# Modulation columns summed on VectorE instead of TensorE, past the first four chunks of layer 0

## The chip, the cores and the metric

One core of a Trainium2 chip runs the whole program. The metric is device time in microseconds (us) of one execution; lower is better. The profile is of one execution on the same kind of chip, with its own time beside it. TensorE does the matrix products (PE in the profile, and PEld for its weight loads), VectorE is DVE, ScalarE is ACT, GpSimd is POOL, and SyncE (SP) issues most transfers.

## The reference, cut to what matters

The network is two blocks of two layers on 256 tokens of width 1024. Only the first block has the modulation that is changed here: from a conditioning vector `c` (and `c_ctx` for the context tokens, in layer 0 alone) a vector of 9 x 1024 = 9216 numbers is made for each layer, and cut into nine terms (shift, scale and gate of three sub-layers).

```python
silu_c = jax.nn.silu(c)
silu_cx = jax.nn.silu(c_ctx)[None]
for l in range(2):
    mod = (silu_c @ w_mod[l] + b_mod[l]).reshape(B, 9, 1, D)        # w_mod[l] is 1024 x 9216 fp32, 37.7 MB
    x = x + 0.5 * gate0 * swiglu(rms_norm(x, g) * (1 + scale0) + shift0, ffn_w_in[l, 0], ffn_w_out[l, 0])
    if l == 0:                                                       # context only here
        modx = (silu_cx @ w_mod[l] + b_mod[l]).reshape(1, 9, 1, D)
        xc = (the same half-FFN of ctx, with modx)
    x = x + gate1 * mixer(rms_norm(x, g) * (1 + scale1) + shift1)
    x = x + 0.5 * gate2 * swiglu(rms_norm(x, g) * (1 + scale2) + shift2, ffn_w_in[l, 1], ffn_w_out[l, 1])
```

`swiglu(h)` is `(silu(h A) * (h B)) W` with a hidden width of 2816 = 22 x 128. The modulation is a product of one or two vectors with a large matrix: each element of `w_mod` is used once or twice.

## The kernel before

Everything is fp32. A large matrix product is made of three passes over rounded parts: weights are split into `whi` (ScalarE copy, line 97) and `wlo` (VectorE subtraction, line 98), activations likewise, and `projT` (line 152) and `rows_out` (lines 184 to 187) run hi by hi, hi by lo and lo by hi.

A half-FFN (`ffn`, line 367) goes through 22 steps `f` of 128 hidden columns. One step loads 1 MB of `ffn_w_in`, splits it in two blocks (the `a` and the `b` half), runs 24 matmuls into `pa` and 24 into `pb`, makes `silu(a) * b` (ScalarE line 386, VectorE line 387), splits that into `gh` and `gl`, and calls the background function `bg(f)` (line 392). `down` (line 189) stands around it: for each pair of steps it loads 1 MB of `ffn_w_out` and adds the products of each step to four accumulators `yacc`, 12 matmuls a step. In layer 0's first half-FFN the matmuls of `pa` and `pb` have 512 columns (tokens and context together), in the other three 256.

The modulation is a generator, `mod_gen(l)` (lines 293 to 331), that is drained from outside. It handles 18 chunks of 512 columns for a layer, two chunks at a time: nine groups, each of four loads of 1 MB (two DMAs of 512 KB, line 308, rows of 2 KB a partition). For each load four matmuls run beside each other on 32 columns of the array each (line 310), with the silu vectors as stationary operand and the weights as the moving one. After the fourth load of a group VectorE copies the 128 x 512 result out of PSUM (`mrow`, line 315), four TensorE transposes turn it into columns (line 318), and a few small VectorE instructions add the bias (lines 326 to 330). One `yield` follows each load, so there are 36 drains a layer.

Who drains: the first eight steps of layer 0 are drained before the first half-FFN (lines 1400 and 1406), while x, context and the first weights arrive; steps 9 to 36 of layer 0 two per `f` from f = 2 to f = 15 of layer 0's first half-FFN (line 1426); layer 1 (`m1`) once in three of four steps `f` of layer 0's second half-FFN (17 drains, line 1458), and once a step in layer 1's first half-FFN (the other 19, line 1468). Layer 1's second half-FFN (line 1484) has the same shape as these two and no background at all. The gate row of a half-FFN is made at f = 14 (`gate`, line 333).

The modulation's load buffer has the tag `raw` in pool `wp`, with two buffers (`RAW`, line 25) that it shares with the loads of `ffn_w_out`; the first eight loads use a pool of six of their own. In layer 0's first half-FFN the `ffn_w_in` weights have two raw buffers and two of `whi` and `wlo` (one step's worth); in the three 256-column ones three raw and four of each (two steps' worth).

The order of the instructions on each engine and queue is set when the program is built: the framework's planner takes the work in the order of the code, and lets a later instruction go first where by its own estimate the earlier one is not ready. On the chip that order is fixed, and each engine waits at its next instruction.

Of the kernel before, what the change touches and what calls it, by code (L numbers as in the profile page):

```python
# [7 lines left out]
F32 = mybir.dt.float32  # L8
# [3 lines left out]
ALU = mybir.AluOpType  # L12
# [3 lines left out]
P = 128  # L16
# [8 lines left out]
RAW, HL = 2, 4  # L25
# [35 lines left out]
class Net:  # L61
# [220 lines left out]
    def mod_setup(self):  # L282
        nc, A = self.nc, self.A
        cc = self.b1.tile([P, KD, 2], F32, name="cc")
        nc.sync.dma_start(cc, A["cc"])
        self.cs = self.b1.tile([P, KD, 32], F32, name="cs")
        nc.vector.memset(self.cs, 0.0)
        nc.scalar.activation(self.cs[:, :, 0:2], cc, AF.Silu)
        self.ng = self.load(self.b1, "ng", [P, 2, 3, KD])
        self.bmc = self.load(self.b1, "bmc", [P, 2, 9, KD])  # L290
        self.mcol = [self.b1.tile([P, 9, 2, KD], F32, name=f"mcol{l}") for l in range(2)]

    def mod_gen(self, l, pool=None):

        nc, A = self.nc, self.A
        v = nc.vector
        mc = self.mcol[l]  # L300
        wv = A["w_mod"][l].rearrange("(k p) (i n) -> p k i n", p=P, n=512)
        for i, d in [(0, 2), (1, 2)] + [(i, 1) for i in range(4, 18, 2)]:
            ps = self.bank(self.mtags[0], "pmod")
            for h in range(4):
                raw = pool.tile([P, 2, 2, 512], F32, name="rawm") if pool is not None and i < 2 else \
                    self.wp.tile([P, 2, 2, 512], F32, name="rawm", tag="raw", bufs=RAW)
                for k in range(2):
                    nc.sync.dma_start(raw[:, k], wv[:, 2 * h + k, i:i + d + 1:d])
                for q in range(4):
                    nc.tensor.matmul(ps[32 * q:32 * q + 32], self.cs[:, 2 * h + q // 2], raw[:, q // 2, q % 2],  # L310
                                     start=(h == 0), stop=(h == 3), tile_position=(0, 32 * q))
                if h < 3:
                    yield
            m = self.b1.tile([P, 512], F32, name="mrow", tag="mrow", bufs=2)
            v.tensor_copy(m, ps)
            p2 = self.bank(self.mtags[1], "pmc")
            for b in range(4):
                nc.tensor.transpose(p2[:, P * b:P * b + P], m[:, P * b:P * b + P], self.ident)

            src = p2.rearrange("p (b h j r) -> p b h j r", b=4, h=2, j=2)[:, :, :, :, 0:2]  # L320
            u = self.sp.tile([P, 2, 2, 4], F32, name="mu", tag="mu")
            for j in range(2):
                t, a = (i + d * j) // 2, 4 * ((i + d * j) % 2)
                o = mc[:, t, :, a:a + 4]
                bc = lambda a: a.unsqueeze(1).to_broadcast([P, 2, 4])
                v.tensor_tensor(u[:, j], src[:, :, 0, j].rearrange("p b c -> p c b"),
                                bc(self.bmc[:, l, t, a:a + 4]), ALU.add)
                v.tensor_tensor(o, u[:, j], src[:, :, 1, j].rearrange("p b c -> p c b"), ALU.add)
                if t % 3 == 1:
                    v.scalar_tensor_tensor(o, o, 1.0, bc(self.ng[:, l, t // 3, a:a + 4]), ALU.add, ALU.mult)  # L330
            yield
# [983 lines left out]
def emit(tc, A, out, lo=0, hi=99, dbg=None):  # L1315
    nc = tc.nc
    rows = lambda a: a.rearrange("(t p) d -> p t d", p=P)
    kview = lambda a: a.rearrange("(k p) n -> p k n", p=P)
    with ExitStack() as ctx:
# [40 lines left out]
        if lo <= 5:  # L1360
            N.b1 = b1.enter_context(tc.tile_pool(name="b1", bufs=1))
            N.mod_setup()
            m0, m1 = N.mod_gen(0), N.mod_gen(1)
# [10 lines left out]
        if lo <= 1:  # L1374
            with ExitStack() as c0:
# [5 lines left out]
                if lo == 0:  # L1381
                    with tc.tile_pool(name="nm", bufs=4) as np_:
                        with tc.tile_pool(name="m0", bufs=6) as mp:
# [15 lines left out]
                            m0 = N.mod_gen(0, mp)  # L1399
# [147 lines left out]
def layout(I):  # L1547

    f = lambda a: np.ascontiguousarray(a)
    o = {}  # L1550
    o["x"], o["ctx"] = f(I["x"][0]), f(I["ctx"][0])
    o["cc"] = f(np.stack([I["c"][0].reshape(KD, P).T, I["c_ctx"].reshape(KD, P).T], -1))
    o["w_mod"], o["ffn_w_out"] = I["w_mod"], I["ffn_w_out"]
# [121 lines left out]
```

## Time and profile before

| | |
|---|---|
| Median of 3 runs | 2303.45 us (2301.2 to 2306.08) |
| The profiled execution | 2302.42 us, of which the span of the trace is 2300.3 us |
| TensorE busy | 2158.5 us (94%) |
| TensorE weight loads | 1596.5 us (69%, beside matmuls) |
| VectorE busy | 1093.4 us (48%) |
| ScalarE busy | 829.7 us (36%) |
| Mean granted TensorE clock | 0.971 of full speed |
| Data moved | 514.48 MB, mean 224 GB/s |

The span is that of one execution; about 2.1 us of its time lies outside. The shares are means over stages that differ: layer 0's first half-FFN lies at about 56 to 370 us, its second at 696 to 890, layer 1's first at 917 to 1111, layer 1's second at 1293 to 1465, and the second block after that.

### The profile page before, as it was taken

Reading aid. Unit: us, or ns where it says so; the run is one execution under the profiler, and the core shown is the slowest. Engines: PE = TensorE matmul, PEld = TensorE weight load, DVE = VectorE, ACT = ScalarE, POOL = GpSimd, SP = SyncE. Lnnn points to the kernel's source line nnn. Section 1 sums busy time; section 2 is a strip of 40 time slices with the busy share of each in tenths; the row PEclk is TensorE's granted clock in tenths of the full one; section 3 lists DMA queues with packets and bytes.
Section 4 is the critical chain, followed back from the end, with each engine's and each line's share of the span. In section 5 each row is a group of like instructions: output and inputs, shape, how many; then the busy total and the mean of one; then the engine's idle time right before and its main releaser. Section 6 shows DMA issues by size and latency. Waiting matters only on the chain. (4 is left out here: it accounts for less than half of the span.)

```text
span 2300.3 us, 30947 instructions
## 1 busy us (share of the span) xinstructions
PE 2158.5 (94%) x12420; PEld 1596.5 (69%) x12420; DVE 1093.4 (48%) x2276; ACT 829.7 (36%) x1441; POOL 65.0 (3%) x76
## 2 busy tenths in 40 slices
PE   7999999989999999999999999899899969979996
PEld 4777788876878887888899899787433338643332
DVE  5233246644675446444676755666311147641113
ACT  4222235534464435334444544464210014521000
POOL 0000000002000000000000000100000021100000
PEclk9999999999999999999999999999899988989998
DMA  8556553434247666776356455333599955349996
GB/s 314 185 218 239 200 183 135 138 115 65 72 148 260 257 233 234 263 266 253 115 175 242 180 176 191 149 133 133 212 393 421 421 228 210 128 179 393 421 421 251
DMA packets 109067, 514.48 MB, mean 224 GB/s; under 512 B 20656, under 2 KB 22064, under 8 KB 67056
## 3 DMA queue, kind: packets, MB, share of 16 engines
q1 hardware_dynamic: 102736, 502.35, 58.4%
q10 hardware_dynamic: 5024, 5.84, 0.9%
q0 software_dynamic: 1152, 4.19, 0.6%
q8 instruction: 101, 1.65, 0.3%
q14 instruction: 54, 0.44, 0.1%
HBM read 511.30 MB, written 1.05 MB: 223 GB/s over the span
## 5 line engine op out<-in xcount | busy, mean ns | idle before, releaser
L98 DVE TENSOR_TENSOR wlo<-raw,whi 128x1024 fp32r<-128x1024 f32 x421 | 513.5, 1232 | 495.0 <-ACT whi L97 492.3
L97 ACT CAST whi<-raw 128x1024 fp32r<-128x1024 f32 x421 | 434.3, 1047 | 686.2 <-PE pa L152 196.0
L152 PE MATMUL pa<-hh,whi 128*128 128x256 f32 (+1 forms) x720 | 224.7, 312 | 2.7 <-DVE hh L277 2.7
L152 PE MATMUL pa<-hh,wlo 128*128 128x256 f32 (+1 forms) x720 | 222.6, 309 | 0.6 <-DVE wlo L98 0.6
L152 PE MATMUL pa<-hl,whi 128*128 128x256 f32 (+1 forms) x720 | 222.8, 309 | 0.3 <-DVE hl L278 0.3
L152 PE MATMUL pb<-hh,whi 128*128 128x256 f32 (+1 forms) x720 | 221.1, 307 | 0.0
L152 PE MATMUL pb<-hl,whi 128*128 128x256 f32 (+1 forms) x720 | 220.8, 307 | 0.0
L152 PE MATMUL pb<-hh,wlo 128*128 128x256 f32 (+1 forms) x720 | 220.6, 306 | 0.0
L184 PE MATMUL yacc<-whi,gh 128*128 128x512 f32 x440 | 172.2, 404 | 1.8 <-ACT gate L343 1.3
L185 PE MATMUL yacc<-wlo,gh 128*128 128x512 f32 x440 | 169.9, 394 | 0.0
L152 PEld LDWEIGHTS pa<-hh,whi 128*128 128x128 f32 x720 | 138.7, 193 | 24.8 <-ACT gh L97 5.9
L1137 PE MATMUL yp<-mw,hT 128*64 128x512 f32 x512 | 139.5, 598 | 9.5 <-DMA mw<-in_w_dn 8.2
L152 PEld LDWEIGHTS pa<-hl,whi 128*128 128x128 f32 x720 | 138.7, 193 | 10.3 <-DVE hh L277 1.7
L152 PEld LDWEIGHTS pa<-hh,wlo 128*128 128x128 f32 x720 | 138.7, 193 | 8.5 <-issue 0.9
L152 PEld LDWEIGHTS pb<-hh,whi 128*128 128x128 f32 x720 | 137.8, 191 | 6.2
L152 PEld LDWEIGHTS pb<-hl,whi 128*128 128x128 f32 x720 | 137.7, 191 | 6.2
L152 PEld LDWEIGHTS pb<-hh,wlo 128*128 128x128 f32 x720 | 137.5, 191 | 6.2
L187 PE MATMUL yacc<-whi,gl 128*128 128x512 f32 x440 | 139.5, 391 | 0.0
L1106 PE MATMUL pe<-mw,xgY 128*64 128x512 f32 x512 | 122.7, 597 | 9.0 <-DMA mw<-in_w_gu 9.0
L1106 PE MATMUL pe<-mw,xgH 128*64 128x512 f32 x512 | 123.2, 605 | 0.0
L1116 DVE SCALAR_TENSOR_TENSOR sg<-sg,gs,pe 128x512 f32<-128x512 f32 x16 | 12.0, 748 | 233.1 <-PE pe L1106 233.1
L184 PEld LDWEIGHTS yacc<-whi,gh 128*128 128x128 f32 x440 | 81.8, 188 | 48.1 <-issue 21.8
(454 smaller groups left out, 3605.7 us busy)
## 6 DMA issues: line engine op xcount, KB each, us to landing
mw<-in_w_gu SPq DMA_DIRECT2D x128, 1024.0 KB, 18.3
raw<-in_ffn_w_in SPq DMA_DIRECT2D x88, 1024.0 KB, 7.0
rawm<-in_w_mod SPq DMA_DIRECT2D x144, 512.0 KB, 5.2
mw<-in_w_dn SPq DMA_DIRECT2D x64, 1024.0 KB, 19.8
raw<-in_ffn_w_out SPq DMA_DIRECT2D x55, 1024.0 KB, 5.0
raw<-in_mix_wT SPq DMA_DIRECT2D x8, 1024.0 KB, 6.2
raw<-in_sg_wR SPq DMA_DIRECT2D x8, 1024.0 KB, 5.1
raw<-in_sg_wT SPq DMA_DIRECT2D x8, 1024.0 KB, 4.8
```

What stands on the lines that cost most here:

```text
L97: self.nc.scalar.copy(hi, src)
L98: self.nc.vector.tensor_tensor(lo, src, hi.bitcast(F32), ALU.subtract)
L152: self.nc.tensor.matmul(o, w[:, k], h[:, k], start=(k == 0 and i == 0), stop=(k == nk - 1 and i == len(steps) - 1))
L184: mm(y[n], a, whi[:, cs[n]], start=first, stop=False)
L185: mm(y[n], a, wlo[:, cs[n]], start=False, stop=False)
L187: mm(y[n], b, whi[:, cs[n]], start=False, stop=last)
L1106: mm(ps[b:b + CAP], xg[j // 4][:, 4 * c + k, P * (j % 4) + b:P * (j % 4) + b + CAP], w[:, 512 * k:512 * k + 512], start=(c == 0 and k == 0 ...
L1116: v.scalar_tensor_tensor(sg, sg, gs[:, j:j + 1], pss[1], ALU.mult, ALU.mult)
L1137: mm(yp[n][b:b + CAP], hT[:, i, b:b + CAP], w[:, D * k + 512 * n:D * k + 512 * n + 512], start=(i == 0), stop=(i == 3), tile_position=(0, b))
```

## The change

Four things change. The chunks are laid out in memory so that half of a chunk (512 rows, 512 columns, 1 MB) is one DMA with 8 KB in a row for each partition. The first four chunks of layer 0 stay on TensorE, one chunk at a time, with sums by a selecting matrix in place of the transposes. All other chunks go to VectorE: each of the 128 partitions multiplies its weights with its own element of the silu vector and adds to a 128 x 512 sum in a buffer `room`, four instructions for a half chunk and vector; in layer 0's chunks 4 to 9 both vectors are wanted, so eight. A group has four sums (two chunks of two vectors, or four chunks of one; layer 1's last has two chunks). When a group's sums are done, four matmuls with a matrix of ones (beside each other, as the old ones) add them over the partitions, `mrow` is copied out as before, and four small matmuls make the columns. The number of loads, of yields and the drains stay as they were.

```diff
-        wv = A["w_mod"][l].rearrange("(k p) (i n) -> p k i n", p=P, n=512)
-        for i, d in [(0, 2), (1, 2)] + [(i, 1) for i in range(4, 18, 2)]:
-            ps = self.bank(self.mtags[0], "pmod")
-            for h in range(4):
...
-                for k in range(2):
-                    nc.sync.dma_start(raw[:, k], wv[:, 2 * h + k, i:i + d + 1:d])
-                for q in range(4):
-                    nc.tensor.matmul(ps[32 * q:32 * q + 32], self.cs[:, 2 * h + q // 2], raw[:, q // 2, q % 2],
-                                     start=(h == 0), stop=(h == 3), tile_position=(0, 32 * q))
-                if h < 3:
-                    yield
-            m = self.b1.tile([P, 512], F32, name="mrow", tag="mrow", bufs=2)
...
-                nc.tensor.transpose(p2[:, P * b:P * b + P], m[:, P * b:P * b + P], self.ident)
...
+        def load(i, h, pool=None):
+            raw = pool.tile([P, 4, 512], F32, name="rawm") if pool is not None else \
+                self.wp.tile([P, 4, 512], F32, name="rawm", tag="raw", bufs=RAW)
+            nc.sync.dma_start(raw, wv[l, i, h])
+            return raw
+        def columns(ps, sel, parts):
+            m = self.b1.tile([P, 512], F32, name="mrow", tag="mrow")
             v.tensor_copy(m, ps)
             p2 = self.bank(self.mtags[1], "pmc")
             for b in range(4):
+                mm(p2[:, 4 * b:4 * b + 4], m[:, P * b:P * b + P], sel, start=True, stop=True)
+            src = p2[:, 0:16].rearrange("p (b n) -> p n b", n=4)
+            for n, (i, c) in enumerate(parts):
+                t, a = i // 2, 4 * (i % 2)
+                o = self.mcol[l][:, t, c, a:a + 4]
+                v.tensor_tensor(o, src[:, n], self.bmc[:, l, t, a:a + 4], ALU.add)
                 if t % 3 == 1:
+                    v.scalar_tensor_tensor(o, o, 1.0, self.ng[:, l, t // 3, a:a + 4], ALU.add, ALU.mult)
+        todo = list(range(18))
+        if l == 0:
+            for i in (0, 2, 1, 3):
+                ps = self.bank(self.mtags[0], "pmod")
+                for h in range(2):
+                    raw = load(i, h, pool)
+                    for q in range(4):
+                        mm(ps[32 * q:32 * q + 32], self.cs[:, 4 * h + q], raw[:, q], start=(h == 0), stop=(h == 1),
+                           tile_position=(0, 32 * q))
+                    if h == 0:
+                        yield
+                columns(ps, self.msum[:, 0], [(i, 0), (i, 1)])
+                yield
+            todo = todo[4:]
+        while todo:
+            both = l == 0 and todo[0] < 10
+            chunks, todo = (todo[:2], todo[2:]) if both else (todo[:4], todo[4:])
+            parts = [(i, c) for i in chunks for c in range(1 + both)]
+            room = acc()
+            for i in chunks:
+                for h in range(2):
+                    raw = load(i, h)
+                    for k in range(4):
+                        for n, (j, c) in enumerate(parts):
+                            if j != i:
+                                continue
+                            o, w = room[:, n], self.cs[:, 4 * h + k, c:c + 1]
+                            if h == 0 and k == 0:
+                                v.tensor_scalar(o, raw[:, k], w, None, ALU.mult)
+                            else:
+                                v.scalar_tensor_tensor(o, raw[:, k], w, o, ALU.mult, ALU.add)
+                    if (i, h) != (chunks[-1], 1):
+                        yield
+            ps = self.bank(self.mtags[0], "pmod")
+            for n in range(4):
+                mm(ps[32 * n:32 * n + 32], self.msum[:, 2, 0:1].to_broadcast([P, 32]), room[:, min(n, len(parts) - 1)],
+                   start=True, stop=True, tile_position=(0, 32 * n))
+            columns(ps, self.msum[:, 1], parts)
             yield
...
-            m0, m1 = N.mod_gen(0), N.mod_gen(1)
+            acc = lambda tag: lambda: N.hp.tile([P, 4, 512], F32, name="macc", tag=tag)
+            m0, m1 = N.mod_gen(0, acc=acc("yl")), N.mod_gen(1, acc=acc("macc"))
...
+    o["w_mod"] = I["w_mod"].reshape(2, 2, 4, P, 18, 512).transpose(0, 4, 1, 3, 2, 5)
```

`msum` is a small constant that is loaded at the start: two selecting matrices and a column of ones. `room` has one buffer.

## Rows read from the trace of the kernel before

**Rows 1.** The page: busy time of TensorE and others; GB/s in 40 slices.

```profile
PE 2158.5 (94%) x12420; PEld 1596.5 (69%) x12420; DVE 1093.4 (48%) x2276; ACT 829.7 (36%) x1441; POOL 65.0 (3%) x76
...
GB/s 314 185 218 239 200 183 135 138 115 65 72 148 260 257 233 234 263 266 253 115 175 242 180 176 191 149 133 133 212 393 421 421 228 210 128 179 393 421 421 251
```

**Rows 2.** Windows: length, busy time (instructions) of each engine, clock, DMA share, GB/s.

```profile
75.06:171.47 96.41, 96.41 (x472) 70.32 (x468) 32.02 (x53) 23.37 (x31) 0.00 (x0) 1.00 0.61 229
171.47:302.21 130.74, 130.29 (x641) 95.79 (x634) 44.96 (x73) 35.34 (x46) 0.00 (x0) 1.00 0.63 233
302.21:329.48 27.27, 27.27 (x122) 22.56 (x121) 10.57 (x14) 7.98 (x11) 0.00 (x0) 1.00 0.33 116
695.86:889.83 193.97, 193.97 (x1390) 168.19 (x1384) 93.87 (x127) 76.97 (x106) 0.00 (x0) 1.00 0.71 256
917.01:1111.13 194.12, 194.12 (x1390) 168.06 (x1389) 94.72 (x134) 75.68 (x105) 0.00 (x0) 1.00 0.69 253
1292.67:1464.75 172.08, 172.08 (x1242) 163.18 (x1241) 93.53 (x106) 78.25 (x106) 0.00 (x0) 1.00 0.52 182
10.00:33.00 23.00, 20.35 (x94) 6.72 (x92) 7.85 (x19) 4.05 (x7) 0.00 (x0) 0.85 1.05 396
```

**Rows 3.** The modulation's load tile: matmuls that read it, and its DMA landings.

```profile
L310 PE MATMUL pmod<-rawm,cs x576: 592/592/1063, 8.8 to 1089.7; 128*32 128x512 f32 x192
...
DMA to landing us min/median/max: 3.6/5.2/12.0
```

**Rows 4.** Timeline of TensorE: start, length, line, out<-in, shapes, count [idle before].

```profile
106.72 0.39 PE L152 MATMUL pb<-hh,wlo 128*128 128x512 f32 x1
107.04 1.92 PE L310 MATMUL pmod<-rawm,cs 128*32 128x512 f32 x16
108.89 0.50 PE L184 MATMUL yacc<-whi,gh 128*128 128x512 f32 x1
...
126.13 0.60 PE L318 MATMUL pmc<-ident,mrow 128*128 128x128 f32 x4
...
270.12 2.05 PE L341 MATMUL pg<-ident,mcol 128*128 128x128 f32 x16
```

**Rows 5.** Timeline of VectorE, one step f of layer 0's first half-FFN.

```profile
107.22 0.42 DVE L387 TENSOR_TENSOR sa<-sa,pb 128x256 f32<-128x256 f32 x1 [3.42 <-PE pb L152]
107.56 0.41 DVE L390 TENSOR_TENSOR gc<-sa,pb 128x256 f32<-128x256 f32 x1
108.00 1.23 DVE L98 TENSOR_TENSOR wlo<-raw,whi 128x1024 fp32r<-128x1024 f32 x1
109.14 0.42 DVE L98 TENSOR_TENSOR gl<-sa,gh 128x256 fp32r<-128x256 f32 x1
118.29 1.23 DVE L98 TENSOR_TENSOR wlo<-raw,whi 128x1024 fp32r<-128x1024 f32 x1 [8.73 <-ACT whi L97]
122.94 0.42 DVE L387 TENSOR_TENSOR sa<-sa,pb 128x256 f32<-128x256 f32 x1 [3.42 <-PE pb L152]
```

**Rows 6.** Timeline of VectorE elsewhere: the nearest rows to the new instructions.

```profile
8.83 0.88 DVE L721 TENSOR_SCALAR xn<-x,rq_t 128x512 f32<-128x512 f32 x2
...
372.93 0.69 DVE L355 TENSOR_TENSOR rtmp<-yacc,gate 128x512 f32<-128x512 f32 x1 [0.46 <-PE yacc L187]
373.54 0.20 DVE L244 TENSOR_SCALAR ss<-ss 128x1 f32<-128x1 f32 x1
373.66 0.69 DVE L356 TENSOR_TENSOR x<-x,rtmp 128x512 f32<-128x512 f32 x1
...
2294.87 2.07 DVE L1541 SCALAR_TENSOR_TENSOR x<-x,rq_t,ln_b 128x512 f32<-128x512 f32 x3
```

**Rows 7.** Timeline of VectorE in layer 1's second half-FFN, the one without background.

```profile
1344.69 1.23 DVE L98 TENSOR_TENSOR wlo<-raw,whi 128x1024 fp32r<-128x1024 f32 x1 [1.30 <-ACT whi L97]
1347.48 1.23 DVE L98 TENSOR_TENSOR wlo<-raw,whi 128x1024 fp32r<-128x1024 f32 x1 [1.57 <-ACT whi L97]
```

**Rows 8.** The page's DMA issues: count, KB each, median us to landing.

```profile
raw<-in_ffn_w_out SPq DMA_DIRECT2D x55, 1024.0 KB, 5.0
```

More of the change, by code (lines that the diff above doesn't have):

```diff
@@ L291, in mod_setup, with mod_gen @@
         self.mcol = [self.b1.tile([P, 9, 2, KD], F32, name=f"mcol{l}") for l in range(2)]
[L293 to L300, printed above, removed]
-        wv = A["w_mod"][l].rearrange("(k p) (i n) -> p k i n", p=P, n=512)
-        for i, d in [(0, 2), (1, 2)] + [(i, 1) for i in range(4, 18, 2)]:
-            ps = self.bank(self.mtags[0], "pmod")
-            for h in range(4):
-                raw = pool.tile([P, 2, 2, 512], F32, name="rawm") if pool is not None and i < 2 else \
-                    self.wp.tile([P, 2, 2, 512], F32, name="rawm", tag="raw", bufs=RAW)
-                for k in range(2):
-                    nc.sync.dma_start(raw[:, k], wv[:, 2 * h + k, i:i + d + 1:d])
-                for q in range(4):
-                    nc.tensor.matmul(ps[32 * q:32 * q + 32], self.cs[:, 2 * h + q // 2], raw[:, q // 2, q % 2],
-                                     start=(h == 0), stop=(h == 3), tile_position=(0, 32 * q))
-                if h < 3:
-                    yield
-            m = self.b1.tile([P, 512], F32, name="mrow", tag="mrow", bufs=2)
+        self.msum = self.load(self.b1, "msum", [P, 3, 4])
+    def mod_gen(self, l, pool=None, acc=None):
+        nc = self.nc
+        v, mm = nc.vector, nc.tensor.matmul
+        wv = self.A["w_mod"]
+        def load(i, h, pool=None):
[5 more added lines that the diff above has]
+            m = self.b1.tile([P, 512], F32, name="mrow", tag="mrow")
             v.tensor_copy(m, ps)
@@ L317, in mod_gen @@
             for b in range(4):
-                nc.tensor.transpose(p2[:, P * b:P * b + P], m[:, P * b:P * b + P], self.ident)
[L320 to L328, printed above, removed]
-                if t % 3 == 1:
-                    v.scalar_tensor_tensor(o, o, 1.0, bc(self.ng[:, l, t // 3, a:a + 4]), ALU.add, ALU.mult)
+                mm(p2[:, 4 * b:4 * b + 4], m[:, P * b:P * b + P], sel, start=True, stop=True)
@@ L1398, in emit @@
                             N.mtags = "CD"
-                            m0 = N.mod_gen(0, mp)
+                            m0 = N.mod_gen(0, mp, acc("yl"))
                             drain(m0, 4)
@@ L1552, in layout @@
     o["cc"] = f(np.stack([I["c"][0].reshape(KD, P).T, I["c_ctx"].reshape(KD, P).T], -1))
-    o["w_mod"], o["ffn_w_out"] = I["w_mod"], I["ffn_w_out"]
+    o["w_mod"] = I["w_mod"].reshape(2, 2, 4, P, 18, 512).transpose(0, 4, 1, 3, 2, 5)
+    o["ffn_w_out"] = I["ffn_w_out"]
+    msum = np.zeros((P, 3, 4), np.float32)
+    for q in range(4):
+        msum[32 * q, 0, 0] = msum[32 * q + 1, 0, 1] = msum[32 * q, 1, q] = 1
+    msum[:, 2] = 1
+    o["msum"] = msum
     o["bmc"] = I["b_mod"].reshape(2, 9, KD, P).transpose(3, 0, 1, 2)
```

## The prediction

> **What bounds the kernel now.** First the page: TensorE is busy 94% of the span and no other engine over half [rows 1]. A mean over stages proves little, so next the windows, cut at the same instruction (line 387) of the half-FFNs. In all six half-FFN windows TensorE is busy for the whole length, at a clock of 1.00, and moved data are 71% of the DMA engines' time at most [rows 2]. So in these stages a microsecond taken off TensorE is one off the span, if nothing else comes to stand there. Only the stage before the first half-FFN is different: from 10 to 33 us DMA is full (396 GB/s) and TensorE's clock is 0.85 [rows 2].
>
> The price of the modulation can be read without a model, because the same half-FFN runs with and without it. Layer 1's second half-FFN takes 172.08 us from its first to its last step. The two with modulation take 193.97 and 194.12 [rows 2]: 21.9 + 22.0 = 43.9 us for layer 1's 36 loads and nine groups. In layer 0's first half-FFN two steps without modulation take 27.27, so 13.64 each; f = 2 to 7 take 96.41, f = 8 to 15 take 130.74 [rows 2]. One of the latter holds the gate row, 16 matmul instructions for 2.05 us [rows 4], some 1.8 of it inserted. The modulation costs 96.41 - 81.8 = 14.6 and 130.74 - 109.1 - 1.8 = 19.8 there. In all 78.3 us lie on TensorE's path: the ceiling of the gain. The timeline shows them: the matmuls of two loads stand between two steps, and the next matmul starts 2.17 us after the last one of before, which is 1.94 more than the 0.23 between neighbours [rows 4]; the rest is four transposes a group (0.60 in the row) and gaps around them.
>
> **What comes back on TensorE.** Ten groups (five in layer 0, five in layer 1) each have four ones-matmuls of the form of line 310. A load's four took 0.97 (half of the above; the 576 instructions of 288 matmuls [rows 3] show that a matmul is two). Then come four matmuls of 128 x 128 by four columns, which no row shows; they are not transposes, so I count two instructions each. The nearest rows are 2.05 for 16, or 1.0 for eight, and 0.60 for four [rows 4]. I take 1.0, the row with two instructions a matmul: 2.0 us a group, 20 in all (bounds 1.6 and 3.0 a group, the latter with a wait for VectorE's copy in front).
>
> **What VectorE gets.** Chunks 4 to 9 of layer 0 are 6 x 2 x 8 = 96 products, chunks 10 to 17 are 64, layer 1 has 144: 304 instructions. Three instructions of this form, with a per-partition scalar and SBUF operands, take 2.07 us [rows 6]; if one lasts 0.74, they start 0.66 apart. The first of each sum multiplies alone: 0.88 for two, so 0.44 [rows 6]. With one vector each adds to the sum that the one before wrote. A dependent pair shows 372.93 + 0.69 = 373.62 and the next at 373.66 [rows 6], 0.04 after the end; so 0.78 for those. With two vectors the sums alternate, and 0.66 holds.
>
> The Trainium skill (VectorE: DVE Perf Modes, section The DRAIN you can't avoid) has a rule against this: after each operation a flush of about its duration less 266 ns, before the next starts. By it 0.74 would become 1.22, and the 304 products some 370 us in place of about 215. The three instructions above started 0.66 apart, inside each other's duration, so the row speaks against the rule for instructions that nothing holds.
>
> A step f of layer 0's first half-FFN has on VectorE, by starts: 0.34 + 0.44 + 1.14 + 0.34 (lines 387, 390, 98, 98), a second 1.14 for the other block [rows 5], and half of the two 1.14 of `ffn_w_out`: 4.5 us.
>
> *f = 2 to 7, both vectors.* Two loads a step are 14 x 0.66 + 2 x 0.44 = 10.1. A group (every second step) adds the copy (0.69, as from PSUM in [rows 6]) and four to eight small ones of about 0.2: 0.7 a step. VectorE needs 15.3 us a step; TensorE 13.64 + 1.0 = 14.6. VectorE becomes the bound: 92 us for the six steps at least, 88 by TensorE alone. Worse is the order: the sums come ahead of the next step's splits in the code, and here there is only one step's worth of `whi` and `wlo`, so block `b` of step f+1 can be split only when `pb` of step f is done. In the row that split comes 0.78 after the start of line 387 [rows 5]. Behind 16 sums it ends at 0.8 + 10.1 + 1.1 = 12.0, while `pb` would want it after 12 + 24 matmuls of 0.23, at 8.2. TensorE waits 3.8, and the step is 12.0 + 5.5 = 17.5: 105 us for six. But the second load often has no buffer yet (two, shared with `ffn_w_out`; 5 us to land, 5 to be summed [rows 3, 8]), and the split slips in. I take the middle, 99 us: 2.6 lost against 96.4.
>
> *f = 8 to 15, one vector.* Eight sums of 0.78 are 6.2; VectorE has 11 us of work in 14. The split ends at 0.8 + 6.2 + 1.1 = 8.1, just as TensorE wants it. 8 x 13.64 + 1.8 + 2 x 2.0 = 114.9, plus 2 for small waits: 116.9, a gain of 13.8 (bounds 15.8 with none, 4 with 1.5 more a step).
>
> *Layer 1.* A step is 8.50 us without modulation and holds about 4.3 of VectorE (93.53 busy over 22 steps [rows 2]). One load adds 3.1: 7.4 in 8.5. Splits run a step ahead there, and the idle in front of them is 1.30 and 1.57 [rows 7], waiting for ScalarE, not late. So TensorE should hardly feel it: 33.9 = 43.9 - 5 x 2.0, less 0.1 a load for misjudged orders, 30.5. Bounds 33.9 and 12, the latter with 0.6 a load: the shared buffer is released about 3 us later than by matmuls, and the `ffn_w_out` load that follows comes later by that.
>
> *The start.* 16 loads of 512 KB are 8.4 MB: 21.2 us at the 396 GB/s of 2 KB rows [rows 2], 19.9 at the 421 that the best slices show [rows 1]. Gain 1.3, less four groups in place of two behind their loads (0.3): 1.0 (bounds +4, if the clock dip goes with it, and -3, if the four copies in series are seen). SP issues half as many DMAs; `mrow` with one buffer and `room` with one order the groups after each other, which costs a wait only where a group's matmuls come late.
>
> **Sum.** -2.6 + 13.8 + 30.5 + 1.0 = 42.7 off the profiled execution's 2302.4, which is 1 us from the median: 2260.
>
> **The rivals.**
> A (the forecast): TensorE freed, VectorE binding only at f = 2 to 7. Own range 2248 to 2273, from 99 +- 6, 1.6 to 3.0 a group and 0 to 0.2 a load. 0.57.
> B: VectorE's queue hides everything, because the planner puts the splits first. 96.4 - 87.8 + 15.8 + 33.9 + 4 = 62: 2240. For it: 8.73 us idle before a split [rows 5]. Against it: 15.3 us of VectorE in 14.6. 0.12.
> C: the two raw buffers bind. Each holds a load through landing and sums, and `ffn_w_out` comes late, so its additions do. f = 2 to 7 at 105 (-9), f = 8 to 15 at a gain of 7, layer 1 at 17, start 0: 15 off, 2287. For it: two loads of 5.3 + 5 and half a load of 8 for `ffn_w_out` make 14 us a step on two buffers. 0.19, of which 0.03 is within 0.2% of before.
> D, slower: the sums stand in front of splits that TensorE waits for, in layer 1 too, and wait turns into wait: TensorE idles at each load. The ceiling less the groups is 78 - 20 = 58 us for 64 loads, so it decides at 0.9 us a load. At 1.3 (under half of layer 1's 3.1 block) it is 83 lost: 2327. For it: fixed order. Against it: the covers of [rows 7]. 0.08.
> E, slower: a sum holds VectorE for longer than it shows, up to a row of twice its width, 1.23 [rows 5], because the next starts only when the one before has left the engine. f = 2 to 7 then need 4.5 + 0.7 + 16 x 1.23 = 24.9 a step (+53), f = 8 to 15 some 14.9 (-10 with the gate), layer 1 4.3 + 4.9 + 0.3 = 9.5 (36 x 1.0 against 43.9: -8): 2337. Against it: the starts in [rows 6]. 0.04. The skill's rule above would make this one come true.
>
> **How the numbers follow.** About 0.2% (4.6 us) is what a measurement of this kernel can tell from no change. Faster: A, B and C without its 0.03 = 0.85; within 0.2%: 0.03; slower: D and E = 0.12. The likeliest is A, 2260. The range takes in A, B's value and most of C: 2239 to 2294.
>
> **What would show it.** Right: line 310's matmuls past 60 us gone and ten ones-rounds in their place; steps of layer 1 near 8.6 to 9.0; VectorE over 80% busy at f = 2 to 7 with steps of 15 to 17.5, and 14 to 14.7 at f = 8 to 15; sums 0.66 apart with two vectors and 0.78 with one; products' total near 215 us. Wrong: TensorE waiting for `wlo` or for `ffn_w_out` in layer 1 (C or D), a granted clock under 1.00 there, which would add to any wait, or sums more than a microsecond apart (E).

## The result, and the profile after

| | Before | After |
|---|---|---|
| Median | 2304.76 us (4 runs beside after's) | 2231.62 us (2228.52 to 2237.53, 4 runs) |
| Ratio | 1 | 0.9687, 95% interval 0.9662 to 0.9711 |
| Profiled execution, its span | 2302.42, 2300.3 | 2237.53, 2235.4 |

The kernel got faster, as forecast, but by 73 us (69 in a second measurement, below), where 43 were forecast and 63 was the most that the range allowed. The page, as in [rows 1]:

```profile
PE 2085.6 (93%) x12028; PEld 1578.7 (71%) x12028; DVE 1283.9 (57%) x2554; ACT 830.2 (37%) x1441; POOL 65.6 (3%) x76
...
GB/s 323 202 238 276 244 113 151 119 118 59 76 154 318 288 280 200 291 296 193 151 170 207 210 206 151 182 114 170 226 404 421 422 222 186 136 203 392 420 421 251
```

TensorE lost 73 us of busy time and VectorE gained 190. The windows of [rows 2], between the same instructions (the multiplication that was line 387):

```profile
76.31:167.30 90.99, 90.99 (x415) 71.50 (x415) 82.89 (x139) 23.12 (x31) 0.00 (x0) 1.00 0.65 234
167.30:281.62 114.32, 114.32 (x524) 92.62 (x523) 81.35 (x119) 35.13 (x46) 0.00 (x0) 1.00 0.69 255
281.62:309.01 27.39, 27.39 (x122) 22.53 (x121) 9.53 (x13) 7.90 (x11) 0.00 (x0) 1.00 0.33 116
677.83:850.06 172.23, 172.23 (x1274) 161.16 (x1273) 132.35 (x179) 77.59 (x106) 0.00 (x0) 1.00 0.78 284
880.26:1056.02 175.76, 174.58 (x1290) 162.24 (x1289) 136.25 (x186) 76.64 (x106) 0.00 (x0) 1.00 0.75 274
1235.28:1401.24 165.96, 165.96 (x1242) 157.07 (x1241) 93.44 (x107) 78.25 (x106) 0.00 (x0) 1.00 0.53 189
10.00:33.00 23.00, 17.31 (x104) 8.90 (x105) 9.23 (x24) 5.16 (x10) 0.00 (x0) 0.86 1.01 421
```

The surprise is the sixth line. Layer 1's second half-FFN has no modulation, before or after, and its code is untouched; yet it takes 165.96 us in place of 172.08 [rows 2], at the same clock of 1.00. The operations are the same and TensorE is busy all the time in both, so the same matmuls must follow each other more closely. TensorE's timeline there, of before and then of after (start, length, line, tiles):

```profile
1302.34 0.28 PE L152 MATMUL pa<-hh,whi 128*128 128x256 f32 x1
1302.46 0.28 PE L152 MATMUL pa<-hl,whi 128*128 128x256 f32 x1
1302.58 0.28 PE L152 MATMUL pa<-hh,wlo 128*128 128x256 f32 x1
1302.70 0.28 PE L152 MATMUL pa<-hh,whi 128*128 128x256 f32 x1
```

```profile
1302.42 0.28 PE L152 MATMUL pa<-hh,whi 128*128 128x256 f32 x1
1302.53 0.28 PE L152 MATMUL pa<-hl,whi 128*128 128x256 f32 x1
1302.65 0.28 PE L152 MATMUL pa<-hh,wlo 128*128 128x256 f32 x1
1302.76 0.28 PE L152 MATMUL pa<-hh,whi 128*128 128x256 f32 x1
```

Three in 0.36 us before, three in 0.34 after. Over all neighbours of this stage the mean distance of two starts is 0.1198 and 0.1138 us. A step has 48 of them: 0.29 us, which is what a step lost (8.50 to 8.21). Nothing in the diff touches these instructions. What it does change is small tiles ahead of them: in the pool `b1`, `mrow` has one buffer for two and `msum` came, and in the pool `sp` `mu` is gone; and so everything behind them lies elsewhere in SBUF. By the compiled program, the `hh` of these half-FFNs starts at byte 54496 of a partition before and 52384 after: 96 and 32 modulo 128. The split weights `whi` stay at 96.

The second timeline is VectorE's in the first half-FFN, after:

```profile
120.17 0.41 DVE L419 TENSOR_TENSOR sa<-sa,pb 128x256 f32<-128x256 f32 x1
...
121.77 1.22 DVE L98 TENSOR_TENSOR wlo<-raw,whi 128x1024 fp32r<-128x1024 f32 x1
...
123.38 1.22 DVE L98 TENSOR_TENSOR wlo<-raw,whi 128x1024 fp32r<-128x1024 f32 x1
124.51 0.88 DVE L353 TENSOR_SCALAR macc<-rawm,cs 128x512 f32<-128x512 f32 x2
125.31 8.69 DVE L355 SCALAR_TENSOR_TENSOR macc<-rawm,cs,macc 128x512 f32<-128x512 f32 x13
135.11 0.42 DVE L419 TENSOR_TENSOR sa<-sa,pb 128x256 f32<-128x256 f32 x1 [1.11 <-PE pb L152]
...
136.78 2.36 DVE L98 TENSOR_TENSOR wlo<-raw,whi 128x1024 fp32r<-128x1024 f32 x2
139.05 0.88 DVE L353 TENSOR_SCALAR macc<-rawm,cs 128x512 f32<-128x512 f32 x2
```

The two splits stand ahead of the block of sums, though the code has the sums first. 13 sums that alternate between two tiles take 8.69, so they start (8.69 - 0.75)/12 = 0.66 apart. With one vector they stand 0.79 apart, (3.11 - 0.75)/3:

```profile
159.32 3.11 DVE L355 SCALAR_TENSOR_TENSOR macc<-rawm,cs,macc 128x512 f32<-128x512 f32 x4
```

And a group on TensorE: eight instructions of the ones-matrix, some matmuls of the step, eight of the columns:

```profile
206.83 1.06 PE L360 MATMUL pmod<-macc,msum 128*32 128x512 f32 x8
...
209.43 1.05 PE L316 MATMUL pmc<-msum,mrow 128*128 128x4 f32 x8
```

The load tile, against [rows 3]: 72 loads of 1 MB as before, in half as many DMAs, landing in 4.7/5.7/15.2.

```profile
L355 DVE SCALAR_TENSOR_TENSOR macc<-rawm,cs,macc x266: 739/749/755, 53.0 to 1022.5; 128x512 f32<-128x512 f32 x133
...
L353 DVE TENSOR_SCALAR macc<-rawm,cs x38: 474/480/490, 50.4 to 1011.9; 128x512 f32<-128x512 f32 x38
...
DMA to landing us min/median/max: 4.7/5.7/15.2
```

### The profile page after: what moved, and what is told of

It is laid out like the page before. It is cut to its first block, busy times and chain, and to the rows that moved or that the text cites. A ratio compares the mean times of both kernels' runs of the same rounds, so it can differ in the third digit from the quotient of the medians.

```text
span 2235.4 us, 30410 instructions
## 1 busy us (share of the span) xinstructions
PE 2085.6 (93%) x12028; PEld 1578.7 (71%) x12028; DVE 1283.9 (57%) x2554; ACT 830.2 (37%) x1441; POOL 65.6 (3%) x76
## 5 line engine op out<-in xcount | busy, mean ns | idle before, releaser
L355 DVE SCALAR_TENSOR_TENSOR macc<-rawm,cs,macc 128x512 f32<-128x512 f32 x266 | 193.2, 748 | 11.2 <-DMA rawm<-in_w_mod 6.9
## 6 DMA issues: line engine op xcount, KB each, us to landing
mw<-in_w_gu SPq DMA_DIRECT2D x128, 1024.0 KB, 18.5
```

The lines of the kernel that those rows point to most:

```text
L355: v.scalar_tensor_tensor(o, raw[:, k], w, o, ALU.mult, ALU.add)
```

## The experiments

Two theories had to be kept apart: that the extra 28 us are TensorE's time that VectorE hides better than forecast, and that part of them has nothing to do with the modulation and comes from the place of tiles in SBUF. A pad is a small tile that nothing reads; it moves what lies behind it.

### The place of the activations: b_pad64, b_pad128, a_pad64

In the kernel before (b_pad64: n = 16, b_pad128: n = 32) and in after (a_pad64: n = 16), behind the line of `mcol`:

```diff
+        self.pad = self.b1.tile([P, n], F32, name="pad")
+        self.nc.gpsimd.memset(self.pad, 0.0)
```

> The kernel before with one 64-byte tile more per partition behind mcol (its only other work: one memset on GpSimd), so that the activations hh and hl of the half-FFNs start at 32 instead of 96 modulo 128 bytes; the modulation stays on TensorE. Placement theory: the 256-column matmuls of lines 152 start 0.113 to 0.118 us apart in place of 0.120, steps of layer 1's second half-FFN take 8.2 to 8.4 us in place of 8.50, and the whole is 12 to 25 us faster than before (about 2280 to 2292). Rival, that the faster spacing comes from the changed work (column matmuls gone, sums on VectorE): 0.120 and 8.50 stay, and the time stays within 5 us of before.

> The same with a tile of 128 bytes: every later tile moves, but hh and hl start again at 96 modulo 128. Placement modulo 128: spacing 0.120, steps of 8.50, time within 5 us of before. If any shift of addresses does it (a collision with one particular neighbour), it is faster like the 64-byte one.

> The changed kernel with the 64-byte tile: hh and hl go back from 32 to 96 modulo 128, all else of the change stays. Placement theory: spacing back to 0.120, layer 1's second half-FFN back to 8.50 a step, 12 to 25 us slower than the changed kernel's 2231.6, so about 2244 to 2257, which is inside what the prediction of record counted for VectorE hiding its work. Rival (changed work): time stays at 2229 to 2237.

Measured: b_pad64 2293.14 us, ratio to before 0.9967 (0.9953 to 0.9981); b_pad128, the control with the old place modulo 128, 2302.45, ratio 1.0012 (1.0003 to 1.0022); a_pad64 2247.87, ratio 0.9768 (0.9751 to 0.9784). In a_pad64 the matmuls stand 0.120 apart again and layer 1's second half-FFN takes what it took before, to the hundredth:

```profile
78.25:169.10 90.85, 90.85 (x416) 71.62 (x415) 82.88 (x138) 23.23 (x31) 0.00 (x0) 1.00 0.66 235
677.42:853.68 176.26, 176.26 (x1274) 165.36 (x1273) 133.06 (x179) 77.97 (x107) 0.00 (x0) 1.00 0.77 279
884.61:1063.09 178.48, 178.48 (x1290) 166.50 (x1289) 136.62 (x186) 76.37 (x106) 0.00 (x0) 1.00 0.73 268
1241.98:1414.06 172.08, 172.08 (x1242) 163.19 (x1241) 93.47 (x106) 78.80 (x107) 0.00 (x0) 1.00 0.51 183
```

So 64 bytes that nobody reads are worth 16 us, and the change itself, with the activations at before's place, 52 to 53 (before ran at 2300.04 and 2302.05 beside its two measurements). a_pad64 is therefore the kernel that the prediction's steps are held against. b_pad64 gained 7 only (0.1178 apart), between its theory (12 to 25) and its rival (at most 5), though its `hh` starts at 32 as in after; the table below comes back to this.

### All chunks on TensorE, in the new layout: pe_all

```diff
-        if l == 0:
-            for i in (0, 2, 1, 3):
+        if True:
+            for i in (0, 2, 1, 3, *range(4, 18)):
...
-            todo = todo[4:]
+            todo = []
```

> The changed kernel with all 36 chunks on TensorE, one chunk at a time (two loads of 1 MB in 8 KB runs, then the small column matmuls); no sums on VectorE. Addresses of hh and hl as in the changed kernel. It holds the new layout and placement but not the move to VectorE. By my sum: placement gains 12 to 25, 8 KB runs about 1, but 36 groups instead of 18 add about 18 x 1.0 of column matmuls in the saturated stages, so 2280 to 2300; the rest to 2231.6, 50 to 65 us, is then the move to VectorE. Rival, that the 8 KB runs or the smaller number of transfers carry a good part of the gain: under 2265.

Measured: 2308.12 us, ratio 1.0034 (1.0019 to 1.0048), with `hh` at the place that it has in after (layer 1's second half-FFN 165.60 us). f = 2 to 7 take 100.06 and f = 8 to 15 135.13, longer than in [rows 2]. That is 8 us above the range of its theory, and far from the rival's 2265: the layout and the work chunk by chunk bring nothing alone. Against pe_all the products on VectorE are worth 76 us, but pe_all has 36 groups where before has 18, so the 52 to 53 of a_pad64 are the better measure. No kernel has the sums with the old layout; what the layout gives beside them is not shown.

### Is VectorE the bound at f = 2 to 7? one_vec

```diff
-                            if j != i:
+                            if j != i or (both and c == 1):
                                 continue
...
-                mm(ps[32 * n:32 * n + 32], self.msum[:, 2, 0:1].to_broadcast([P, 32]), room[:, min(n, len(parts) - 1)],
+                mm(ps[32 * n:32 * n + 32], self.msum[:, 2, 0:1].to_broadcast([P, 32]), room[:, n - n % 2 if both else min(n, len(parts) - 1)],
```

> The kernel after with hh and hl moved back by a 64-byte tile (a_pad64, so that the 256-column matmuls stay 0.120 us apart), and in chunks 4 to 9 of layer 0 only the sums of the first vector: 4 per load in place of 8. Left out: the context's modulation from those chunks (the ones-matrix round reads the first vector's sum twice). Theory: in the steps f = 2 to 7 VectorE is the bound (82.9 us busy of 90.85), and what it can't do there is done in the step f = 8 (18 us against 14). Then six steps fall to TensorE's own 14.2 to 14.4 us, f = 2 to 8 from 90.85 to about 86, f = 8 to 16 from 113.6 to about 112, the start by 1 us or so, as the first sums stand between splits there too: total 2248 to about 2241. Rival: TensorE, or the landing of the 8 KB runs, is the bound in these steps, and VectorE only looks full: each of the three stretches stays within 1 us, total 2246 to 2250.

Measured: with the context's modulation left out the values that reach the expert layers are others, and these load 480 blocks of weights in place of 192; the total, 3102.65, says nothing. The stages ahead of it:

```profile
81.16:168.78 87.62, 87.62 (x408) 70.13 (x407) 60.07 (x100) 21.01 (x29) 0.00 (x0) 1.00 0.64 236
168.78:283.66 114.88, 114.88 (x530) 93.81 (x529) 78.81 (x115) 34.99 (x46) 0.00 (x0) 1.00 0.66 247
```

f = 2 to 7 fell by 3.2 us, less than the theory's 5, and f = 8 to 15 rose by 1.3: together from 204.4 (90.85 + 113.56 in a_pad64) to 202.5. Taking half of the two-vector sums away is worth 1.9 us over fourteen steps. Most of the shift between the two stretches is TensorE's own, because its additions to `yacc` don't keep to the steps. At f = 2 to 7 a_pad64 and then one_vec have of them (the window's length, then TensorE's matmuls on `yacc`, their weight loads):

```profile
78.25:169.10 90.85, 20.06 (x80) 14.27 (x79) 0.00 (x0) 1.00 0.66 235
81.16:168.78 87.62, 18.00 (x72) 12.67 (x71) 0.00 (x0) 1.00 0.64 236
```

So 2 of the 3.2 us are eight additions that one_vec does later. The long step that ends this stretch in a_pad64 (18.5 us, with 12.2 behind it) is no backlog of VectorE either: it holds 20 additions, the next one 7, and TensorE idles in neither. VectorE was 83 us busy of 91 and still hardly the bound. Neither theory is met as it was put; what holds of the rival is that TensorE is the bound but for 1.9 us. The start did not get shorter (81.16 against 78.25), but its granted clock from 35 to 76 us was 0.90, against 1.00 in a_pad64.

### How much room VectorE has in layer 1: l1_half, l1_twice

```diff
-                            if j != i:
+                            if j != i or (l == 1 and k % 2):
```

```diff
                                 v.scalar_tensor_tensor(o, raw[:, k], w, o, ALU.mult, ALU.add)
+                            if l == 1:
+                                v.scalar_tensor_tensor(o, raw[:, k], w, o, ALU.mult, ALU.add)
```

> a_pad64 with every second sum of layer 1 left out (k = 0 and 2 only; layer 1's modulation is then that of half the rows): same loads, same ones-matrix rounds, half the work on VectorE. The two half-FFNs with layer 1's chunks take 176.3 and 178.5 us against 172.1 without modulation, 10.6 us in all. Theory: these are the ones-matrix rounds and column matmuls on TensorE (4.5 rounds of some 2 us), the sums being hidden: both stretches stay within 1 us, total within 2 us of 2248. Rival: sums that run late hold the splits in some steps (steps of 9.3 and 12.4 us stand beside steps of 8.5): each stretch falls by 2 us or more, total 2243 or less.

> a_pad64 with each sum of layer 1 done twice (layer 1's products count double): 7 or 8 sums per load for 4, same loads and rounds. VectorE is busy 133 and 137 us of 176 and 178 in the two half-FFNs that carry them; 18 loads x 4 x 0.787 us are 57 us more, 190 and 193 in all. Theory: VectorE's room is 40 us a half-FFN, more than the change uses but less than twice it, so each half-FFN gets longer by at least 14 us and by up to 30 where the loads come unevenly: total 2276 to 2308. Rival: the room is larger than the busy time says, since these steps wait for TensorE anyway: under 6 us each, total below 2260.

Measured: l1_half 2244.38 us, ratio 0.9755 (0.9739 to 0.9772). The two half-FFNs take 176.23 and 178.10, against 176.25 and 178.48: half of the sums gone, and they are as long as before. What they cost above 172.08 is TensorE's groups: two in the first (4.2 us), three in the second (6.4), 2.1 each. The total is 3 us lower by the ratios, whose intervals overlap; the trace puts 2.2 between the two half-FFNs and 1.6 in the start.

l1_twice 2288.56, ratio 0.9942 (0.9925 to 0.9959): some 40 us longer, inside the theory's range, but not spread as it said. Its two windows:

```profile
677.21:863.25 186.04, 185.71 (x1297) 170.15 (x1297) 171.20 (x241) 77.03 (x105) 0.00 (x0) 1.00 0.73 267
891.75:1103.31 211.56, 194.17 (x1300) 171.99 (x1299) 187.01 (x266) 77.41 (x106) 0.00 (x0) 0.98 0.63 233
```

The first took in its extra sums for 10 us, and TensorE hardly waits; 24 of its matmuls on `yacc` (242 against 218) are work that a_pad64 does behind the window, and with the stretch behind it it is some 7 longer. The second is 33 us longer: TensorE is idle for 17 of them, at a clock of 0.98 (the other 16 are not split up here), and its waits, of which a_pad64 has none in this stretch, are on the sums and on what is queued behind them (line numbers are two to four higher here):

```profile
PE pmod L364 <- DVE macc L359: 6.1, 1, 6.1
PE pa L152 <- ACT sa L422: 5.3, 5, 1.3
PE yacc L184 <- ACT whi L97: 4.0, 3, 2.0
```

So VectorE's room is there and ends between once and twice the load that the change puts on it.

### What the place acts on: a_pad96, a_pad32, a_wshift, a_both, a_rel, a_rel64, a_rel0

The pad in `b1` moves the activations (n = 24 in a_pad96, a_both and a_rel0, 8 in a_pad32 and a_rel64, 16 in a_rel). A second pad in a pool of its own moves the weights (m = 24 in a_wshift, a_both and a_rel64, 16 in a_rel, 8 in a_rel0):

```diff
+        wpad = self.ws.enter_context(self.tc.tile_pool(name="wpad", bufs=1, side="right"))
+        self.nc.gpsimd.memset(wpad.tile([P, m], F32, name="wpad"), 0.0)
         self.wp = self.ws.enter_context(self.tc.tile_pool(name="wp", bufs=1, side="right"))
```

> The kernel after with a 96-byte tile in the pool of hh and hl: they start at 0 mod 128 bytes (32 in after, 96 in a_pad64 and in the kernel before). Theory: the spacing of the 256-column matmuls goes by where the moving operand starts in a span of 128 bytes, and a start at 0 is at least as good as 32: 0.113 to 0.118 us apart, steps of 8.2 to 8.45 us, total 2225 to 2238. Rival: only 32 is good, or it is the distance to other buffers and not the start that counts: 0.120 apart, steps of 8.50, total 2246 to 2250.

> The kernel after with a 32-byte tile, that is with hh and hl at 64 mod 128 bytes (0: 0.117, 32: 0.113 or 0.118, 96: 0.120 us apart). Theory: 0 and 64 are alike, the spacing goes by the start in a span of 64 bytes up to 32, and 96 is the odd one: 0.117, steps of 8.4 us, 2239 to 2246. Rival: the later the start in 128 bytes the slower, 64 between 32 and 96: 0.119 to 0.120, steps of 8.5 us, 2246 to 2250.

> The kernel after with the pool of the weights shifted by 96 bytes: the split weights whi and wlo start at 0 mod 128 bytes in place of 96; hh and hl stay at 32. whi and wlo are the moving operand of the 512-column matmuls (the yacc products and others) and the stationary one of pa and pb. Theory: only the narrow 256-column matmuls feel where their moving operand starts, since the 512-column ones stay 0.227 us apart whether it starts at 0, 32 or 96; nothing changes, 2229 to 2238. Rival: the 512-column matmuls lose time to a start at 96 as well, some 0.004 to 0.007 us each of 0.227; some 1,400 of them in the FFNs alone, 6 us or more: 2215 to 2226.

> The kernel after with both shifts of 96 bytes: hh and hl at 0 mod 128 (0.117 us in a_pad96, 2242.6 us in all), and whi and wlo at 0 mod 128. Theory: as in a_pad96, 2239 to 2246, since the weights' place does nothing. Rival: what counts is where operands start relative to each other or to the weights, then the spacing of the 256-column matmuls falls to 0.113 or rises to 0.120 with hh where it was: 2225 to 2232, or 2246 and more.

> The kernel after with hh and hl at 96 mod 128 bytes (as in a_pad64 and in the kernel before, where the 256-column matmuls stood 0.120 us apart) and the split weights shifted by 64 bytes, to 32. So far, by hh's start less the weights' start, mod 128: 0 (before, a_pad64) 0.120; 0 (a_both) 0.119; 32 (a_pad96 and a_wshift, by two ways) 0.117 in both; 96 (a_pad32) 0.118; 64 (after) 0.113 or 0.118. Theory: what counts is the distance between the moving operand and the weights; here it is 64 again: 0.113 or 0.118, steps of 8.21 or 8.45 us, total 2228 to 2240. And pj of the attention, whose H stays at 32, is now at a distance of 0: from 0.114 in after to 0.119 or 0.120. Rival: hh's own start decides, and 96 is the bad one: 0.120, steps of 8.50, total 2246 to 2250, pj as in after.

> The kernel after with hh and hl at 64 mod 128 bytes and the split weights at 0: a distance of 64, by another way than after (32 and 96, which is 64 round the span of 128) and a_rel (96 and 32). Theory: distance alone: 0.113 to 0.118 us, below the 0.1183 of a_pad32 with the same hh; total 2229 to 2246, and if 0.113 comes with every distance of 64, near 2232. Rival: hh at 64 stays at 0.1183 whatever the weights' place, 2248.

> The kernel after with hh and hl at 0 mod 128 bytes and the split weights at 64: again a distance of 64. Theory: as a_rel64, 0.113 to 0.118 us, 2229 to 2246; with a_rel64 it tells whether 0.113 is had by a distance of 64 or by after's addresses alone. Rival: as in a_pad96 with the same hh, 0.1168, 2242.

The table has, by the compiled programs, the start of `hh` and of `whi` modulo 128, their difference modulo 128 and modulo 256; and layer 1's second half-FFN, with the mean distance of two starts of its 256-column matmuls, worked out from all neighbours in the trace. The code of this stage is the same in all of them.

| Kernel | hh | whi | hh - whi, mod 128 | hh - whi, mod 256 | spacing, us | half-FFN, us | median, us |
|---|---|---|---|---|---|---|---|
| before | 96 | 96 | 0 | 0 | 0.1198 | 172.08 | 2303.45 |
| b_pad128 | 96 | 96 | 0 | 128 | 0.1187 | 171.43 | 2302.45 |
| a_pad64 | 96 | 96 | 0 | 0 | 0.1199 | 172.08 | 2247.87 |
| a_both | 0 | 0 | 0 | 128 | 0.1188 | 171.56 | 2250.16 |
| a_pad96 | 0 | 96 | 32 | 32 | 0.1167 | 169.77 | 2242.56 |
| a_wshift | 32 | 0 | 32 | 32 | 0.1167 | 169.79 | 2241.91 |
| b_pad64 | 32 | 96 | 64 | 64 | 0.1178 | 170.93 | 2293.14 |
| a_rel | 96 | 32 | 64 | 64 | 0.1178 | 170.90 | 2245.57 |
| a_rel64 | 64 | 0 | 64 | 64 | 0.1178 | 170.90 | 2248.11 |
| a_rel0 | 0 | 64 | 64 | 64 | 0.1178 | 170.90 | 2241.43 |
| a_pad32 | 64 | 96 | 96 | 224 | 0.1183 | 171.44 | 2248.42 |
| after | 32 | 96 | 64 | 192 | 0.1138 | 165.95 | 2231.62 |

My first theory, that the start of the moving operand `hh` decides, fell with a_both and a_wshift: with `hh` left where it was, moving the weights alone took the spacing from 0.1167 to 0.1188 and from 0.1138 to 0.1167. Its second form, that the difference decides, then said 0.113 or 0.118 for a_rel, which has `hh` at the 96 that had always been the slow place; it came out at 0.1178, and so did a_rel64 and a_rel0. (Where an expectation called the weights' place idle, or a start of 64 like one of 0, it missed.) Modulo 128 the difference thus orders the kernels with two exceptions: after, which has 64 and 0.1138, and b_pad128 and a_both, which have 0 and 0.1187 where before and a_pad64 have 0.1198. Modulo 256 none is left: kernels of one difference agree to 0.0001 us, and after has 192 where the four at 0.1178 have 64. The attention's `pj`, whose `H` lies elsewhere, bears this out: 0.1144 us at 192 (before and b_pad128; 0.1156 in b_pad64), 0.1172 at 64 (after), 0.1189 at 128 (a_rel, whose expectation said 0.119 or 0.120, but took 0.114 for after's). This order was found in the finished table; no kernel was run to try it, and 192 and 224 rest on one place of `hh` each. The totals of neighbours in the table differ by several us by other stages, the start above all, and aren't the measure of this; those of a_pad96, a_rel and a_rel64 lie above the range of a theory whose spacing came true.

### Is after's spacing its own? after_again, a_pad64_again

Both unchanged, beside a_rel64 and a_rel0 on one chip.

> The kernel after, unchanged, once more and beside a_pad64 on one chip. Theory: the spacing goes by its addresses alone: 0.113 to 0.118 us with the same changes at the column blocks of layer 1's modulation, about 2232 us, 14 to 17 us below a_pad64. Rival: the 0.113 came from the chip or the run: 0.118 throughout, about 2243 us, within 6 us of a_pad64.

> a_pad64 unchanged, once more beside after: 0.120 us and about 2248 us, as before, by either theory; it is the mark for after_again.

Measured: 2232.60 us, ratio 0.9695 (0.9682 to 0.9709), and 2249.15, ratio 0.9771 (0.9756 to 0.9786). The 16.5 us between them are there again, and layer 1's second half-FFN takes 165.95 and 172.08 once more. In this stage it is after's addresses, not the chip or the run. Elsewhere the addresses alone don't settle it: in layer 0's second half-FFN matmuls 0.113 and 0.118 apart are mixed in both executions of the same program (mean 0.1157 and 0.1151), and they change over at different places, mostly at the groups' column matmuls. What makes them change over stays open.

## Why the prediction was right in its direction and short in size

Stages of the profiled executions, as differences from before, beside the terms of the sum:

| Stage | forecast | a_pad64 | after |
|---|---|---|---|
| to f = 2 | -1.0 | +3.2 | +1.3 |
| f = 2 to 7 | +2.6 | -5.6 | -5.4 |
| f = 8 to 15 | -13.8 | -17.2 | -16.4 |
| f = 16 to layer 0's second FFN | 0 | +1.1 | +2.6 |
| layer 0's second and layer 1's first half-FFN, with the stretches behind them | -30.5 | -32.3 | -39.4 |
| layer 1's second half-FFN | 0 | 0.0 | -6.1 |
| the rest | 0 | -3.5 | -1.4 |
| sum | -42.7 | -54.2 | -64.9 |

(Medians: 52 to 53 us for a_pad64, 69 to 73 for after; after's profiled execution was its longest.) The rest is no term: kernels alike up to there have between 830 and 836 us in it.

*What put the time out of its range* is a term that the sum did not have. It took every matmul of the FFNs to keep its spacing (the steps of 8.50 us without modulation), since none of them was edited. The change moved the activations in SBUF, and the 256-column matmuls follow each other 0.004 to 0.006 us sooner: 16 us of median between a_pad64 and after. In the profiled executions 12.9 of it lie in the three half-FFNs of 256 columns (13.2 in the second pair); where the rest lies is not shown. Without it the forecast's range holds, at 2248, the lower end of A's own range. The next miss had a part in it: with the 8 us of f = 2 to 7 on top, after would have been at 2240, just inside.

*f = 2 to 7* was mis-sized by 8, and two steps failed. One is the order. I let the sums stand ahead of the splits, as the code has them, and took the middle, 99. The schedule put the splits first, as B said, and TensorE waited for none of them (in a_pad64 it is busy for 90.85 of 90.85). The other is the count: I put all 96 sums with two vectors into these six steps. In a_pad64 23 of layer 0's 160 sums ran before f = 2, 82 here and 55 behind, so that the 92 by VectorE was no floor. The 88 by TensorE was (87.62 in one_vec). The order of this kernel's loop could not be read as the order on the chip; the idle 8.73 before a split in [rows 5] was the better evidence.

*f = 8 to 15*: 113.6 against 116.9; the 2 us for small waits did not come, and five of its additions to `yacc`, 1 us of work, ran before f = 8 (92 here, 97 before). Over both stretches TensorE's own floors, 88 + 114.9 = 202.9, met 202.5 in one_vec and 204.4 in a_pad64.

*Layer 1*: the two half-FFNs lost 17.7 + 15.6 = 33.4 us of their 43.9 in a_pad64. The floor was 33.9 with 2.0 a group; a group cost 2.1, so nothing that shows was lost to misjudged orders: the 0.1 a load was too much (for 36 loads it would also have made 30.3, not 30.5). l1_half shows it from the other side. The stretches behind gave back 1.1. That steps would be 8.6 to 9.0 was wrong in form: in layer 1's first half-FFN the second to sixth are 8.50 like those without modulation, the seventh, with a group, is 10.6, and the later ones scatter between 7.6 and 12.4 but for two short ones at the end.

*The groups*: 1.0 + 1.0, as the nearest rows had it.

*The sums*: 0.66 and 0.79 us apart, as [rows 6] had it for 0.66 and 0.78 (for the 0.78 with some luck: another instruction stands between that pair), and 266 x 0.749 + 38 x 0.480 = 217 us in all against 215. E, which needed starts of more than a microsecond apart, fell with it. By an estimate from the Trainium skill's rule (VectorE: DVE Perf Modes, The DRAIN you can't avoid) the next would have started 0.749 + 0.483 = 1.23 after the last. The same section of the Trainium skill excepts an instruction that is not held; the trace agrees with the exception, with 0.66 and, where each sum needs the one before, 0.79. The 370 us that the prediction has by that rule count the 38 shorter first products like the rest; by the same estimate it is some 350.

*The start* went the other way, +1.3 to +3.2 (in one_vec, at the lower clock, +6.1). The loads did move at 421 GB/s in place of 396, but the last column of chunk 3 came at 36.8 us against 35.5 before (38.5 in a_pad64): four groups in series, with four waits of TensorE for the copy into `mrow` (4.2 us, against two and 1.6 before), were the price that the bound of -3 stood for. That is nearly all of it: from that column to f = 2 it is 39.6 us before, 39.5 in after and 39.8 in a_pad64. In this stretch what had been excluded did come true, sums between splits:

```profile
50.01 0.43 DVE L277 CAST hh<-hm 128x512 fp32r<-128x512 f32 x1 [1.43 <-ACT hm L275]
50.35 0.48 DVE L353 TENSOR_SCALAR macc<-rawm,cs 128x512 f32<-128x512 f32 x1
50.75 0.69 DVE L278 TENSOR_TENSOR hl<-hm,hh 128x512 fp32r<-128x512 f32 x1
51.35 0.42 DVE L277 CAST hh<-hm 128x512 fp32r<-128x512 f32 x1
51.69 0.48 DVE L353 TENSOR_SCALAR macc<-rawm,cs 128x512 f32<-128x512 f32 x1
```

Each `hh` and `hl` is wanted by the next matmuls, and a sum of 0.5 to 0.7 us stands before four of the `hl` (the code takes the first sum at f = 2, the schedule has it at 50 us). TensorE shows no loss by it: from 36 to 62 us it waited 0.9 us for `hh` and `hl` in after, 2.0 before.

*The rivals.* B had the mechanism at f = 2 to 7; with TensorE's time it gave 2240, and 2248 is between A and B. C and D did not come: in the half-FFNs that carry the sums TensorE waits for no `wlo` and no `ffn_w_out` (its only idle there is 1.1 us in after, for an `mrow`). Two raw buffers were enough, as 0.78 of DMA time in layer 0's second half-FFN still left no wait on TensorE.

## What to carry to other kernels

Work that is taken off the engine that binds can be worth nearly its whole time (52 to 53 us here, of 58 that could be had), as long as the engine that gets it can do it within the same steps; busy time of 91% did not make VectorE the bound, and only twice the load in layer 1 made TensorE wait. Cut stages at the same instruction and look also at stages that the change doesn't touch: one that got faster at the same clock, with the same instructions, says that the gain isn't all the change's. Whoever adds or drops a tile should run a control with a pad that restores the old addresses before he credits the difference to the edit.

## What the runs showed of the hardware

A 256-column fp32r matmul, stationary 128 x 128, that follows its like at a clock of 1.00 starts 0.1138 to 0.1199 us after it, by where the two operands lie: the same instructions, up to 5%. In the twelve kernels of the table this goes by the difference of the two starts modulo 256 bytes. The 512-column `yacc` of the same stage, where the weights are the moving operand, start 0.229 (before, a_pad64, after) to 0.233 us apart (a_rel, a_wshift, a_pad96); so in these last three a part of what the narrow ones gain is given back, and in after none. Layer 0's first half-FFN can't show it: there the weights lie in a pool behind the activations and move with them. The Trainium skill (TensorE: Matmul & The Clock Gate, Step-by-step: what each phase is for) says that the stationary and the moving operand have read ports of their own and that a load of weights takes nothing from a running matmul. By that alone the place of the weights would not matter to `pa` and `pb`, in which `whi` and `wlo` are only stationary. Here it did: in a_wshift only the weights' pool moved (with the raw loads that it also holds), and the spacing went from 0.1138 to 0.1167. That the two reads meet in SBUF would explain it, but no run here measures such a meeting; it is argued, not shown.
